# Gate projections of a hybrid attention encoder: 768 full products, or 56 half-size products in two passes

## The chip, the core and the metric

The kernel is one program on one core of a Trainium2 chip. A core has TensorE (PE: matrix products out of SBUF into PSUM), VectorE (DVE), ScalarE (ACT), GpSimd (POOL) and SyncE (SP, which here issues all DMAs). Each engine works through its own list of instructions in order; semaphores hold an instruction back until its inputs are there. Time is device time in microseconds of one execution, the median of several; less is better.

## The reference

One encoder block over 1024 tokens of width 1024 with 16 learned meta tokens put in front (1040 keys), float32. The normed input `h` is projected by `w_in` to the queries, keys and values of two attention branches and to two gates, each 1024 wide:

```
proj = h @ w_in                      # qa ka va | qb kb vb | ga gb
y_a = differential_attention(qa, ka, va)   # 4 heads, all keys, alibi bias; no distance for meta keys
y_b = windowed_gqa(qb, kb, vb)             # 8 heads, window 128 plus the meta keys
merged = sigmoid(ga) * (y_a @ w_ba) + sigmoid(gb) * (y_b @ w_bb)
h = h + merged @ w_o
h = h + (silu(n @ w_gate) * (n @ w_up)) @ w_down,   n = rms_norm(h)
```

Only the 1024 real tokens are returned, so the gates are needed for these alone.

## The kernel before

Every product is made in float32r in three terms: both operands are split into a high part (ACT copies it, rounding) and a low part (DVE or POOL subtracts), and high x high, high x low, low x high are added up in PSUM (`split`, L111). The normed input lies transposed in SBUF as `hT_hi`, `hT_lo` (8 blocks of 128 channels by 1040 tokens) from the start until the gates are done.

**Projections** (L193 to L232, L492 to L533). A column block of `w_in` of 128 columns is loaded (`w_c`), split by ACT and POOL into `wh_c`, `wl_c` (`prep`, L169, two buffers each in `wpool`), and multiplied with the tokens in chunks; a chunk is 8 steps of three matmuls. Results go through `stage` (tile `qk_stage`, three buffers) to HBM, since branch A's operands don't fit beside branch B's. `order` lists the column blocks in the order of use, `ensure` prepares the next one while the present one runs; the 16 gate blocks stand at its end. Branch B (`attend_b`, `units_b`) runs in between, in two groups; the projections of branch A's heads fill PE while a unit of branch B waits for its softmax. In this part the order on all engines is worked out when the program is built, by a planner that goes by the order of writing and by what is ready.

**Branch A and the gates** (L551 to L739). Here PE's order is written out by hand. For each of 4 heads and 8 tiles of 128 queries, `scores_a` makes two score maps in three key chunks (`A_CHUNKS`) each; DVE takes the bias off and keeps the running minimum (L610; the 16 meta keys at the end of the last chunk are a call of their own with `no_dist`), ACT takes the exponential (L615), POOL scales map 1 (L618), DVE joins the maps (L621), POOL copies the meta columns (L622). A tile later the difference is transposed (`transpose_a`), split and multiplied with the values (`values_a`), and each half head is normed (`normed_a`). The gates are the filling: `gate_steps` yields after each step of three matmuls (512 columns each), 8 steps for half a column block, 256 in all; each letter `g` in `SLOTS` (`SLOTS_LAST` for the last head) is one step, 30 (`G_FIRST`) come before head 0 and 10 (`G_HEAD`) before the other heads, to cover `load_a`, and 36 (`HOLD`) are held back for the end. ACT copies each half block out and SP stores it (`g_d`). `gated` (L806) reads them back.

**Pools.** SBUF is given out as two stacks: left `bpool` (branch B), then `apool` (branch A), then `ypool`; right `acon`, `hpool` (hT), `wpool`, `stage`, then `gstage` in the place of `stage`. A pool opened where another was closed takes its memory. Each DMA is one instruction in SP's list.

## Time and profile before

| what | value |
|---|---|
| median of 3 runs | 1461.66 us (1461.31 to 1463.18) |
| profiled execution, its span | 1464.6 us |
| projections and branch B | 66 to 306 us |
| gates alone, loading of head 0 | 306.5 to 327.4 us |
| branch A with gates between | 327.4 to 606 us |
| rest of the gates, last norms | 606 to 642 us |
| merge, output projection, feed-forward | from 642 us |

The profile is of one execution. A row of instructions has the line, the engine, the operation, the tiles (written <- read), shapes and count, then busy time and the mean of one; a median or a mean of a matmul is its whole flight, while matmuls follow one another more closely. Views by window give the busy time of each engine in a stretch; the chain of waits follows the work that ended last backwards, so that its pieces add up to the span. A line can be that of a helper: L112 and L113 are the two halves of every split, L200 every projection's matmul.

### The profile page before, as it was taken

What the parts mean: (1) busy time and instruction counts of PE and PEld (TensorE: products, weight loads), DVE (VectorE), ACT (ScalarE), POOL (GpSimd) and SP (SyncE); (2) the same over time, 40 slices, a digit from 0 to 9 for tenths busy, and PEclk for the clock granted to TensorE, in tenths of its full rate; (3) what the DMA queues carried; (4) which work ended last, traced back from release to release, by engine and by line L of the source; (5) the groups of instructions that cost most, each with busy time, mean ns of one, the idle gap of its engine ahead of it and who ended that gap; (6) DMA issues with size and microseconds to landing.
All of it is one profiled execution on the core that took longest, in us unless ns stands there. A gap on an engine that the chain in (4) does not pass through costs nothing.

```text
span 1464.6 us, 21066 instructions
## 1 busy us (share of the span) xinstructions
PE 1443.4 (99%) x7375; PEld 1238.1 (85%) x7375; DVE 854.9 (58%) x1666; ACT 655.2 (45%) x1237; POOL 534.6 (36%) x502
## 2 busy tenths in 40 slices
PE   8999999999999999999999999999999999999997
PEld 6999989988898999878888878888888888888886
DVE  7355426627786868433513876555555554787667
ACT  6355436525454555444512743333333333444454
POOL 5143223313323232224822565545555442000444
PEclk9999999999999999999999999999999999999999
DMA  7333452372524251077521434323233322954333
GB/s 242 86 95 111 119 131 88 77 209 90 148 77 145 73 153 66 30 261 220 182 106 72 144 109 144 125 98 102 100 108 101 102 100 99 356 188 140 122 127 139
DMA packets 156153, 189.97 MB, mean 130 GB/s; under 512 B 16192, under 2 KB 101632, under 8 KB 156048
## 3 DMA queue, kind: packets, MB, share of 16 engines
q1 hardware_dynamic: 156048, 188.63, 40.5%
q8 instruction: 58, 0.95, 0.3%
q14 instruction: 47, 0.39, 0.1%
HBM read 128.09 MB, written 53.94 MB: 124 GB/s over the span
## 4 chain that ended last, share of the span: by engine, by line
PE 85%; POOL 4%; issue 4%; DMA 3%; DVE 2%; ACT 1%; SPq 1%; POOLq 0%; ACTq 0%; DVEq 0%
PE pg L1092 28%; PE pp_g L200 10%; PE pd L1186 8%; PE po L869 6%; PE ppa L548 4%; PE aps L604 4%; PE apy L646 3%; PE pp_va L200 3%; PE pp_qa L200 3%; PE pp_ka L200 3%; PE pp_qb L200 3%; POOL oa L113 3%; PE apt L633 2%; PE bpt L338 2%; PE bpy L344 2%
## 5 line engine op out<-in xcount | busy, mean ns | idle before, releaser
L1092 PE MATMUL pg<-t,wop 128*128 128x512 f32 x1056 | 242.6, 389 | 0.0
L113 POOL TENSOR_TENSOR wop<-wf,wop 128x512 fp32r<-128x512 f32 x128 | 174.2, 1365 | 164.2 <-ACT wop L112 149.7
L1092 PEld LDWEIGHTS pg<-t,wop 128*128 128x128 f32 x1056 | 198.2, 188 | 41.2
L1186 PE MATMUL pd<-ob,oa 128*128 128x512 f32 x924 | 210.2, 389 | 1.2 <-DVE ob L113 0.7
L1186 PEld LDWEIGHTS pd<-ob,oa 128*128 128x128 f32 x924 | 173.3, 188 | 37.9 <-DVE ob L113 1.2
L1092 PE MATMUL pg<-b,wop 128*128 128x512 f32 x792 | 185.6, 392 | 2.3 <-DVE c L1101 2.3
L1092 PEld LDWEIGHTS pg<-b,wop 128*128 128x128 f32 x792 | 149.4, 189 | 34.2 <-issue 2.4
L113 POOL TENSOR_TENSOR wl_c<-w_c,wh_c 128x1024 fp32r<-128x1024 f32 x32 | 77.6, 2425 | 159.4 <-ACT wh_c L112 134.3
L112 ACT ACTIVATE wop<-wf 128x512 fp32r<-128x512 f32 x128 | 80.3, 632 | 84.2 <-PE pg L1092 52.1
L615 ACT ACTIVATE as<-as,amn 128x1040 f32<-128x1040 f32 x64 | 74.5, 1164 | 73.9 <-DVE amn L610 73.9
L113 POOL TENSOR_TENSOR oa<-ra,oa 128x512 fp32r<-128x512 f32 x33 | 44.0, 1335 | 171.1 <-ACT oa L112 169.7
L200 PE MATMUL pp_g<-hT_hi,wh_c 128*128 128x512 f32 x256 | 101.7, 397 | 0.0
L200 PE MATMUL pp_g<-hT_lo,wh_c 128*128 128x512 f32 x256 | 101.4, 396 | 0.0
L200 PE MATMUL pp_g<-hT_hi,wl_c 128*128 128x512 f32 x256 | 101.3, 396 | 0.0
L112 ACT ACTIVATE oa<-ra 128x512 fp32r<-128x512 f32 x77 | 48.6, 632 | 107.3 <-PE pd L1186 54.6
L604 PE MATMUL aps<-ak,aq 128*128 128x352 f32 (+1 forms) x384 | 93.2, 328 | 0.0
L869 PE MATMUL po<-woh,mT 128*128 128x512 f32 x384 | 88.0, 390 | 0.0
L869 PEld LDWEIGHTS po<-woh,mT 128*128 128x128 f32 x384 | 71.9, 188 | 14.8
L604 PEld LDWEIGHTS aps<-ak,aq 128*128 128x128 f32 x384 | 70.1, 190 | 14.3 <-DVE amn L610 0.2
L927 DVE TENSOR_TENSOR s<-wf,wf 128x512 f32<-128x512 f32 x22 | 18.3, 830 | 107.1 <-DMA wf<-in_w_ff_gate_dram 54.0
L610 DVE CUSTOM_DVE_ANT_0 as<-aps,dist,amn 128x352 f32<-128x352 f32 (+1 forms) x128 | 71.3, 564 | 10.4 <-PE aps L604 8.1
L325 POOL TENSOR_SCALAR bs<-bs,bdn 128x432 f32<-128x432 f32 (+1 forms) x64 | 37.0, 596 | 98.0 <-DVE bdn L323 56.5
(255 smaller groups left out, 2940.4 us busy)
## 6 DMA issues: line engine op xcount, KB each, us to landing
ra<-aop SPq DMA_DIRECT2D x77, 256.0 KB, 2.6
w_c<-in_w_in_dram SPq DMA_DIRECT2D x33, 512.0 KB, 4.0
wf<-in_w_ff_gate_dram SPq DMA_DIRECT2D x24, 512.0 KB, 3.6
wf<-in_w_ff_up_dram SPq DMA_DIRECT2D x24, 512.0 KB, 3.6
aop<-as SPq DMA_DIRECT2D x44, 256.0 KB, 2.1
aop<-c SPq DMA_DIRECT2D x33, 256.0 KB, 2.0
g_d<-gate_stage SPq DMA_DIRECT2D x32, 256.0 KB, 2.0
gt<-g_d SPq DMA_DIRECT2D x32, 256.0 KB, 3.2
```

Of the source, the lines that this page charges most:

```text
L112: nc.scalar.activation(hi, src, AF.Copy)
L113: lo_eng.tensor_tensor(lo, src, f32(hi), ALU.subtract)
L200: nc.tensor.matmul(ps[:, :n], a[:, c, :], b[:, c, at:at + n], start=(c == 0 and i == 0), stop=(c == DC - 1 and i == 2))
L325: nc.gpsimd.tensor_scalar(st[:, r, :W], st[:, r, :W], dn[:, r:r + 1], 1.0, ALU.mult, ALU.mult)
L548: nc.tensor.matmul(ps, w[:, a, j, :], src(j, b, tk), start=(j == 0 and n == 0), stop=(j == 3 and n == 2))
L604: nc.tensor.matmul(ps[:, :n], qs[m][:, t * P:(t + 1) * P], ks[m][:, vv, k0:k0 + n], start=(vv == 0), stop=(vv == 1))
L610: nc.vector.tensor_tensor_reduce(s[m][:, a:b], ps[:, a - k0:b - k0], far_by, slope, low, ALU.add, ALU.min, mn[:, m, i + j:i + j + 1])
L615: nc.scalar.activation(s[m][:, 0:L], s[m][:, 0:L], AF.Exp, bias=low, scale=-1.0, accum_out=dn[:, m:m + 1])
L646: nc.tensor.matmul(py[:, cols], v[:kp, a, k, :], at_[:kp, k, b, :], start=(k == 0 and j == 0), stop=(k == 8))
L869: nc.tensor.matmul(ps, mT[:, c, a, t * P:(t + 1) * P], wos[q, c][:, b], start=(c == 0 and n == 0), stop=(c == DC - 1 and n == 2))
L1092: nc.tensor.matmul(ps, op[:, x, c, :], b[:, y, c, :], start=(p in (1, 2, 5) and c == 0 and n == 0), stop=(p in (4, 2, 3) and c == 3 and n ...
L1186: nc.tensor.matmul(ps[u], oa[:, a, u * P:(u + 1) * P], ob[:, b, :], start=(p in (1, 2, 5) and j == 0 and k == 0), stop=(p in (2, 3, 4) and ...
```

## The change

The gates are made by Winograd's form of Strassen's product: two column blocks (256 columns) of a gate, all 1024 channels and all 1024 tokens are each cut in halves, and seven products of half size (4 steps of 128 channels, three matmuls of 512 columns each) replace eight. The kernel needs sums of weight quarters (POOL, `g_prep`) and sums of token quarters. The latter, 5, 6, 7 and 4, are made once (`token_sums`, on POOL, split by ACT and DVE), in the projections, kept in HBM (`ts_d`) and loaded over quarters of hT that are no longer needed (`load_sums`). Products 2, 5 and 3 of all eight pairs form the first pass and 1, 6, 7 and 4 the second; partial results go to `g_d` and come back (`kept`) to be added by DVE. In all 56 products of 4 steps, 224 steps.

With it go: the gates' weights leave `order`, `wpool` and `stage` are closed before the gates and a new `gpool` takes their place; tiles have four gate steps in all heads; the score chunks become 392, 392 and 256 keys, and the last, with the meta keys in it, uses a copy of the distances with zeros at their place (`dist_m`, made by POOL), so that the separate call goes; the last key projection takes its chunks in reverse order. What is not shown of the diff are the new tiles' declarations in HBM and the removal of `no_dist`.

```diff
@@ -37,11 +37,11 @@
 COMBINE_POOL = (0, 1, 2, 3)
-SLOTS = "sgsgsngsgsgstntnt"
-SLOTS_LAST = "sgsgsngsgsstntnt"
+SLOTS = "sgsgsngsgsstntnt"
 S_BUFS = (2, 2)
...
 G_BUFS = 3
+GV_BUFS = 4
 HOLD = 36
...
@@ -159,7 +161,7 @@
     Q_CHUNKS = [(0, 512), (512, 512)]
-    A_CHUNKS = [(0, 352), (352, 352), (704, 336)]
+    A_CHUNKS = [(0, 392), (392, 392), (784, 256)]
     KB_CHUNKS = [(0, 256), (256, 256), (512, 256), (768, 272)]
@@ -180,7 +182,6 @@
             order += [C_QB + 2 * P, C_QB + 3 * P]
-    order += [C_GB + i * P for i in range(8)] + [C_GA + i * P for i in range(8)]
     prepped = {}
...
@@ -489,6 +488,43 @@
     flush_v()
+    def quad(hl, kh, half):
+        return (hT_hi, hT_lo)[hl][:, 4 * kh:4 * kh + 4, half * 512:half * 512 + 512]
+    tpool, close_tpool = pool("tpool", "right")
+    def token_sums(c):
+        tt = nc.gpsimd.tensor_tensor
+        def new(name):
+            return tpool.tile([P, 512], F32, tag="ta", name=f"ta{name}_{c}", bufs=3)
+        def part(hl, kh, half):
+            return f32(quad(hl, kh, half)[:, c])
+        def keep(p, src):
+            to = tpool.tile([P, 2, 512], F32R, tag="to", name=f"to{p}_{c}", bufs=2)
+            split(to[:, 0], to[:, 1], src, nc.vector)
+            nc.sync.dma_start(ts_d[p][:, :, c, :], f32(to))
+        t1, low = new(1), new("l1")
+        tt(t1, part(0, 0, 1), part(0, 0, 0), ALU.subtract)
+        tt(low, part(1, 0, 1), part(1, 0, 0), ALU.subtract)
+        tt(t1, t1, low, ALU.add)
+        keep(5, t1)
+        t3, t2 = new(3), new(2)
+        tt(t3, part(0, 1, 1), part(0, 0, 1), ALU.subtract)
+        tt(t2, part(1, 1, 1), part(1, 0, 1), ALU.subtract)
+        tt(t3, t3, t2, ALU.add)
+        keep(7, t3)
+        tt(t2, t3, part(0, 0, 0), ALU.add)
+        tt(t2, t2, part(1, 0, 0), ALU.add)
+        keep(6, t2)
+        t4 = new(4)
+        tt(t4, part(0, 1, 0), t2, ALU.subtract)
+        tt(t4, t4, part(1, 1, 0), ALU.add)
+        keep(4, t4)
     def project_a(h):
@@ -509,7 +545,7 @@
         project_v(C_VA + h * P, f"va{h}", va_evac)
-        project(C_KA + h * P, K_CHUNKS, f"ka{h}", evac_split(None, k_consume))
+        project(C_KA + h * P, K_CHUNKS if h < AH - 1 else K_CHUNKS[::-1], f"ka{h}", evac_split(None, k_consume))
@@ -523,8 +559,12 @@
     units_b(0, qb, first_b)
+    for c in range(2):
+        token_sums(c)
     project_a(0)
+    token_sums(2)
     project_a(1)
+    token_sums(3)
     qb = new_qb(1)
@@ -548,21 +588,105 @@
+    close_tpool()
+    close_stage()
+    close_wpool()
+    gpool, close_gpool = pool("gpool", "right")
+    def load_sums(p, kh, half):
+        for hl in range(2):
+            nc.sync.dma_start(f32(quad(hl, kh, half)), ts_d[p][:, hl])
+    load_sums(5, 0, 1)
+    G_ACT = {2: (1, 0), 5: (0, 1), 3: (1, 1), 1: (0, 0), 6: (1, 0), 7: (0, 1), 4: (1, 1)}
+    G_OUT = {2: (0, 0), 5: (1, 1), 3: (0, 1), 1: (0, 0), 6: (0, 1), 7: (1, 1), 4: (1, 0)}
+    order_g = [(2, k) for k in range(4)]
+    for k in range(0, 8, 2):
+        order_g += [(p, k + i) for p in (5, 3) for i in range(2)]
+        if k < 4:
+            order_g += [(2, k + 4 + i) for i in range(2)]
+    for k in range(0, 8, 2):
+        order_g += [(p, k + i) for p in (1, 6, 7, 4) for i in range(2)]
+    g_ready, g_raw, g_kept, g_bank = {}, {}, {}, {}
+    def g_cols(k):
+        return (C_GB, C_GA)[k // 4] + k % 4 * 256
+    def g_tile(name):
+        return gpool.tile([P, 512], F32, tag="gv", name=name, bufs=GV_BUFS)
+    def g_place(p, k):
+        row, half = G_OUT[p]
+        return g_d[2 * k + row][:, half * 512:half * 512 + 512]
+    def g_prep(n):
+        p, k = order_g[n]
+        at, tt = g_cols(k), nc.gpsimd.tensor_tensor
+        def load(out, kh, c0, cn):
+            nc.sync.dma_start(out, w_in[kh * 512:kh * 512 + 512, at + c0:at + c0 + cn].rearrange("(c p) n -> p c n", p=P))
+        if p == 2:
+            src = g_tile(f"g12_{k}").rearrange("p (c n) -> p c n", n=P)
+            load(src, 1, 0, P)
+        else:
+            if p in (5, 1):
+                raw = g_raw[k] = gpool.tile([P, 2, 4, 256], F32, tag="gr", name=f"gr{p}_{k}", bufs=2)
+                load(raw[:, 0], 0, 0, 256)
+                if p == 5:
+                    load(raw[:, 1], 1, 0, 256)
+                else:
+                    nc.sync.dma_start(raw[:, 1, :, 0:P], s2_d[k])
+                    load(raw[:, 1, :, P:256], 1, P, P)
+            raw = g_raw[k]
+            a11, a21, a12, a22 = (raw[:, i, :, j * P:j * P + P] for i in range(2) for j in range(2))
+            if p == 5:
+                tt(a21, a21, a22, ALU.add)
+            elif p == 3:
+                tt(a11, a21, a11, ALU.subtract)
+                nc.sync.dma_start(s2_d[k], a11)
+                tt(a12, a12, a11, ALU.subtract)
+            elif p == 7:
+                tt(a21, a11, a21, ALU.subtract)
+            src = {5: a21, 3: a12, 1: a11, 6: a12, 7: a21, 4: a22}[p]
+            if p in (1, 6, 7):
+                kept = g_kept[p, k] = g_tile(f"gk{p}_{k}")
+                nc.sync.dma_start(kept, g_place(p, k))
+        op = g_ready[p, k] = gpool.tile([P, 2, 4, P], F32R, tag="gop", name=f"gop{p}_{k}", bufs=4)
+        split(op[:, 0], op[:, 1], src, nc.gpsimd)
+    g_prepped = [0]
+    def g_ahead(n):
+        while g_prepped[0] < min(n, len(order_g)):
+            g_prep(g_prepped[0])
+            g_prepped[0] += 1
+    g_ahead(3)
     def gate_steps():
-        for i in range(16):
-            def g_evac(ps, at, n, i=i):
-                st = gstage.tile([P, 512], F32, tag="g", name="gate_stage", bufs=G_BUFS)
-                nc.scalar.copy(st, ps)
-                nc.sync.dma_start(g_d[i][:, at:at + n], st)
-
-            ensure(1)
-            col = (C_GB if i < 8 else C_GA) + (i % 8) * P
-            for _ in project_steps(col, Q_CHUNKS, f"g{i}", g_evac):
+        for n, (p, k) in enumerate(order_g):
+            g_ahead(n + 3)
+            op, act = g_ready.pop((p, k)), G_ACT[p]
+            if p in (2, 5, 1):
+                g_bank[k] = pp_bank(f"pg{p}_{k}")
+            ps = g_bank[k]
+            for c in range(4):
+                for i, (a, b) in enumerate(((0, 0), (0, 1), (1, 0))):
+                    nc.tensor.matmul(ps, op[:, a, c], quad(b, *act)[:, c], start=(p in (2, 5, 1) and c == 0 and i == 0),
+                                     stop=(p in (2, 3, 4) and c == 3 and i == 2), skip_group_check=True)
+                if c == 3:
+                    if p in (1, 6, 7):
+                        st = g_kept.pop((p, k))
+                        nc.vector.tensor_tensor(st, ps, st, ALU.add)
+                    else:
+                        st = gpool.tile([P, 512], F32, tag="g", name="gate_stage", bufs=G_BUFS)
+                        nc.scalar.copy(st, ps)
+                    nc.sync.dma_start(g_place(p, k), st)
+                    if k == 7 and p in (2, 5, 3):
+                        load_sums({2: 6, 5: 7, 3: 4}[p], *act)
                 yield
-            ensure(W_BUFS - 1)
-
-    close_stage()
-    gstage, close_stage = pool("gstage", "right")
     apool, close_apool = pool("apool")
@@ -570,6 +694,12 @@
         nc.gpsimd.memset(s0s[i][:, L + 2 * NM:], 0.0)
+    last_k0 = A_CHUNKS[-1][0]
+    dist_m = apool.tile([P, NT, L - last_k0], F32, name="dist_m")
+    nc.gpsimd.memset(dist_m[:, :, S - last_k0:], 0.0)
+    for t in range(NT):
+        u0 = 896 - t * P
+        nc.gpsimd.tensor_copy(dist_m[:, t, 0:S - last_k0], dist[:, u0 + last_k0:u0 + S])
@@ -603,13 +733,10 @@
                                      start=(vv == 0), stop=(vv == 1))
-                parts = [(k0, min(k0 + n, S), dist[:, u0 + k0:u0 + min(k0 + n, S)])]
-                if k0 + n > S:
-                    parts.insert(0, (S, L, no_dist))
-                for j, (a, b, far_by) in enumerate(parts):
-                    nc.vector.tensor_tensor_reduce(s[m][:, a:b], ps[:, a - k0:b - k0], far_by, slope, low,
-                                                   ALU.add, ALU.min, mn[:, m, i + j:i + j + 1])
-                    low = mn[:, m, i + j:i + j + 1]
+                far_by = dist_m[:, t] if k0 == last_k0 else dist[:, u0 + k0:u0 + k0 + n]
+                nc.vector.tensor_tensor_reduce(s[m][:, k0:k0 + n], ps[:, :n], far_by, slope, low,
+                                               ALU.add, ALU.min, mn[:, m, i:i + 1])
+                low = mn[:, m, i:i + 1]
                 if i < 2:
@@ -671,7 +798,7 @@
-    n_gates = [256 - HOLD]
+    n_gates = [4 * len(order_g) - HOLD]
@@ -715,7 +842,7 @@
             turning = turn(tiles[n - T_LAG])
-        for what in SLOTS if n < 3 * NT else SLOTS_LAST:
+        for what in SLOTS:
             if what == "s":
@@ -739,8 +866,7 @@
     close_psum2()
-    close_stage()
-    close_wpool()
+    close_gpool()
     close_hpool()
```

More of the change, by code (lines that the diff above doesn't have):

```diff
@@ L100, in encoder_block @@
     g_d = [dram.tile([P, S], F32, name=f"g_d{i}") for i in range(16)]
+    ts_d = {p: dram.tile([P, 2, 4, 512], F32, name=f"ts_d{p}") for p in (5, 6, 7, 4)}
+    s2_d = [dram.tile([P, 4, P], F32, name=f"s2_d{k}") for k in range(8)]
     ya_d = [dram.tile([P, S], F32, name=f"ya_d{h}") for h in range(4)]
@@ L465, in encoder_block @@
         nc.gpsimd.memset(tbx[:, j, P:144], 0.0 if j == 1 else FAR)
-    no_dist = acon.tile([P, NM], F32, name="no_dist")
-    nc.gpsimd.memset(no_dist, 0.0)
     far_a = acon.tile([P, 1], F32, name="far_a")
```

## Prediction, written before the changed kernel was run

> **What bounds the kernel now.** I read the page first, for the engine that is never free.
>
> ```profile
> span 1464.6 us, 21066 instructions
> ...
> PE 1443.4 (99%) x7375; PEld 1238.1 (85%) x7375; DVE 854.9 (58%) x1666; ACT 655.2 (45%) x1237; POOL 534.6 (36%) x502
> ...
> PEclk9999999999999999999999999999999999999999
> ```
>
> TensorE (PE) is busy 99% of the span at full clock, so work taken from it is worth its time, and every stall put in front of it costs its time. Then the busy time by stretches (us, then busy us of PE, PE weight loads, DVE, ACT, POOL, the granted clock, DMA share, GB/s), for the two projection stretches before the gates, and the chain of waits for three runs of gate matmuls and for the value matmuls that close each pair of query tiles.
>
> ```profile
> 66.00:178.00 112.00, 111.02 (x667) 101.71 (x666) 61.80 (x148) 60.17 (x145) 34.89 (x46) 1.00 0.39 107
> 178.00:306.00 128.00, 128.00 (x729) 115.48 (x728) 64.19 (x147) 62.92 (x144) 40.02 (x48) 1.00 0.40 107
> 389.77 6.96 PE pp_g L200 x30
> 484.07 1.08 PE apy L646 x9
> 500.41 1.07 PE apy L646 x9
> 570.07 1.07 PE apy L646 x9
> ...
> 600.13 1.08 PE apy L646 x9
> ```
>
> Thirty gate matmuls take 6.96 us on the chain: 0.232 us each, 0.696 us for a gate step of three (the 394 ns of a single record overlaps its neighbours). Two tiles with five gate steps each take 500.41 - 484.07 = 16.34 us; in the last head, with four, four tiles take 600.13 - 570.07 = 30.06. The difference, 8.17 - 7.52 = 0.65 us a tile, is one step: also a tile with four steps is set by TensorE, not by DVE.
>
> Last, the seam between the projections and branch A: the first gate matmuls and the first score matmuls on PE, the DMA issues of SP, and POOL (start, us, line).
>
> ```profile
> 306.50 0.40 PE L200 MATMUL pp_g<-hT_hi,wh_c 128*128 128x512 f32 x1
> ...
> 327.39 0.48 PE L604 MATMUL aps<-ak,aq 128*128 128x352 f32 x2
> 306.17 3.00 SPq L352 DMA_DIRECT2D yb_d<-by  x4
> ...
> 309.97 1.26 SPq L500 DMA_DIRECT2D ka_d<-qk_stage  x2
> 311.32 0.54 SPq L580 DMA_DIRECT2D aq<-qa_d  x1
> 323.78 9.27 DMA w_c<-in_w_in_dram
> 290.76 2.40 POOL L113 TENSOR_TENSOR wl_c<-w_c,wh_c 128x1024 fp32r<-128x1024 f32 x1 [3.36 <-ACT wh_c L112]
> 307.77 2.40 POOL L113 TENSOR_TENSOR wl_c<-w_c,wh_c 128x1024 fp32r<-128x1024 f32 x1 [14.61 <-ACT wh_c L112]
> 310.11 0.27 POOL L572 MEMSET as<- 128x80 f32 x2
> L313 PE MATMUL bps<-kb,qb x128: 288/358/466, 63.8 to 282.1; 128*128 128x432 f32 x96, 128*128 128x288 f32 x32
> q1 hardware_dynamic: 3136, 5.68, 101.6%
> ```
>
> Here PE has no gap: the gates begin as the projections end, because their first weights were split at 290.76 while the last projection ran, in a pool (`wpool`) that lives on; 30 steps (20.9 us) then cover the loading of head 0. But what lies in a newly opened pool starts late. The memset of `as0` stands at 310.11 although POOL idled 14.61 us before 307.77 and the memory was that of `kb0`; `aq` of head 0 is issued at 311.32 although its place was `kb1`, read for the last time near 282.1 (the last score matmul of branch B). A new pool gets its first instruction when the last one of the old pool has gone out, here the `yb_d` stores. And from 311.3 to 331.5 (the last line: packets, MB, share) the DMA engines are full, with 5.68 MB, 281 GB/s; a 512 KB load issued in there at 323.78 takes 9.27 us.
>
> **The change part by part.** *Gate products.* 16 columns x 2 halves x 24 = 768 matmuls become 56 products x 12 = 672: 96 x 0.232 = **-22.3 us** of PE, all of it on the path, since four steps a tile are still PE's. That is 32 gate steps: one fewer in each of 24 tiles of heads 0 to 2, the rest at the end of branch A.
>
> *The seam.* The new `gpool` takes the place of `wpool`, `stage` and `tpool`, so by the two rows above its first load waits for the last `ka_d` store (309.97 + 1.26 = 311.2). Costs of making an operand:
>
> ```profile
> L112 ACT ACTIVATE wop<-wf x128: 615/633/637, 827.9 to 1225.0; 128x512 fp32r<-128x512 f32 x128
> L113 POOL TENSOR_TENSOR wop<-wf,wop x128: 1274/1291/1805, 828.6 to 1225.7; 128x512 fp32r<-128x512 f32 x128
> g_d<-gate_stage SPq DMA_DIRECT2D x32, 256.0 KB, 2.0
> ```
>
> A 256 KB transfer (2.0 to 2.6), ACT's copy 0.63, POOL's rest 1.29 and the hand-overs make 4.7: product (2,0) begins at about 316, where PE was busy from 306.5. Three operands are ordered before `load_a`; (2,3) and the two 1 MB blocks that (5,0) and (5,1) need come behind its 13 issues. Together from 311.3: four 256 KB blocks, 4.1 MB of head 0, 2.1 MB of raw weights, some 1.3 MB of stores: 8.5 MB at 281 GB/s = 30 us, so the last block lands near 341.5. (The token sums' 2 MB go out at about 303, when the reversed K_CHUNKS free their place, into DMA that is idle until 311.) Then POOL has, one behind the other, the sum and split of (5,1), the split of (3,0), and two differences and the split of (3,1): 6 x 1.29 = 7.8; two steps of (3,1) add 1.4. The first scores come at about 351 instead of 327.4: **+23.6 us**. This wait stands at the head of PE's hand-written order, so the scores, whose data have landed, queue behind it. The eight copies that fill `dist_m` (one operand, below 1.29 us each, 10 us in all) fall into POOL's waiting for these loads and cost nothing; without that wait they would. Bounds: 7 us, if only the first operand is late and the rest lands in time; 40 us, if `load_a` goes out wholly before the gate loads, which then start after 331.5 with PE idle till then. I take 23.6, since DMA alone, full, gives it.
>
> *Clock.* PE loses its clock in a wait:
>
> ```profile
> 340.54 1.20 PE L633 MATMUL apt<-ident,as 128*128 128x128 f32 x9 [2.15 <-DVE as L621]
> 342.00:344.00 2.00, 2.00 (x7) 1.71 (x6) 1.86 (x6) 1.62 (x4) 0.38 (x1) 0.50 0.01 1
> 344.00:346.00 2.00, 2.00 (x8) 1.62 (x8) 0.98 (x6) 0.00 (x0) 0.00 (x0) 0.67 0.00 0
> ```
>
> After 2.15 us of idling it ran at 0.50 and 0.67 for 4 us: 2 x 0.50 + 2 x 0.33 = **+1.7 us**, once (a second wait there is followed by more waiting). The Trainium skill, "TensorE: Matmul & The Clock Gate", Part 1, has the clock halved after an idle window of about 3.4 us; the trace shows it after 2.15 us, and by the skill's figure two long waits would cost twice 1.7 us, as an estimate.
>
> *Token sums.* 40 operations on POOL of 1.29 (52 us) and 16 splits on ACT and DVE, in stretches where POOL now works 34.89 + 40.02 of 240 us; 16 stores of 512 KB on SP. They are covered by PE's projections. What is late when POOL is taken are the weight splits that sit behind them; the trace has them ready well ahead:
>
> ```profile
> 73.72 1.95 POOL L325 TENSOR_SCALAR bs<-bs,bdn 128x288 f32<-128x288 f32 x4 [16.50 <-DVE bdn L323]
> 77.87 2.38 POOL L113 TENSOR_TENSOR wl_c<-w_c,wh_c 128x1024 fp32r<-128x1024 f32 x1 [1.85 <-ACT bes L321]
> 90.66 2.09 PE pp_va L200 x12
> ```
>
> 12 of the first 20 fit into POOL's 16.50 us of idleness; the split for `va0` ends at 80.25 and is used at 90.66. They take nothing off the path, so no gain. I take **+2** (0 to 10: one branch B unit's softmax held up by 1.29 us in each of 8).
>
> *Loop of branch A.* DVE's groups (count, busy us, mean ns) in the last head, the addition that resembles the new ones, and the window of two of its tiles:
>
> ```profile
> L610 DVE CUSTOM_DVE_ANT_0 as<-aps,dist,amn 128x352 f32<-128x352 f32 x16 | 9.3, 579 | 2.3 <-PE aps L604 2.0
> L610 DVE CUSTOM_DVE_ANT_0 as<-aps,dist,amn 128x320 f32<-128x320 f32 x16 | 8.8, 547 | 0.3
> L610 DVE DVE_READ_ACCUMULATOR2_ANT amn<- 128x1 f32 x64 | 5.2, 82 | 0.0
> L610 DVE CUSTOM_DVE_ANT_0 as<-aps,no_dist,amn 128x16 f32<-128x16 f32 x16 | 3.7, 229 | 1.3 <-PE aps L604 0.4
> L1106 DVE TENSOR_TENSOR p<-pg,p 128x512 f32<-128x512 f32 x21 | 14.4, 686 | 6.2 <-PE pg L1092 4.7 <-ACT p L1112 1.5
> 572.00:587.00 15.00, 15.00 (x102) 13.95 (x101) 12.98 (x44) 8.25 (x14) 3.08 (x5) 1.00 0.07 24
> ```
>
> 1 ns a column: chunks of 392, 392, 256 cost 619 + 619 + 483 and three reads, where 579 + 579 + 547 + 229 and four stood; 0.3 us less per map, 0.6 per tile. The 24 additions of the second pass (686 ns, one operand in PSUM) put 0.5 back in half of the tiles. DVE stays at its 13 of 15 us. POOL gets one product a tile, 1.29 to 3.9 us; it works 3 of 15 now. With the gates' loads and stores between, and four steps instead of five over each head's loading, DVE's relief gains nothing where PE sets the tile, but it pays for the wait of `L622` or `L618` behind one more POOL operation. I take **+3** (0 to 12) over 32 tiles.
>
> *Tail.* 36 steps are left where 40 were, in front of branch B's loads:
>
> ```profile
> 631.99 9.26 DMA tb<-yb_d
> 642.68 44.29 PE ppa L548 x194
> ```
>
> The load lands at 641.2 and PE goes on at 642.7: the 4 steps saved (2.8 us) are mostly waited out, **+2** (0 to 2.8).
>
> Sum: 1464.6 - 22.3 + 23.6 + 1.7 + 2 + 3 + 2 = 1474.6 for the profiled execution; its span is 2.9 above the median of the runs, 1461.66, so 1471.7.
>
> **Rivals.** *The seam is bridged (faster).* If the order of SP puts the raw blocks of (5,0) and (5,1) ahead of head 0's, or the pool opens earlier, PE loses only the first operand, 7 to 10 us: 1461.66 - 22.3 + 9.6 + 1.7 + 2 + 1 + 2 = 1455.7. For it: weights of g1 and g2 were loaded before `load_a` in the old kernel, whose order follows readiness. Against: those lay in an open pool. It decides where the seam costs under 14 us.
>
> *A wash.* The seam costs 14 to 18: 1461.
>
> *Head 0 first.* The gate loads go out behind all of `load_a`; 40 instead of 23.6: 1488.
>
> *Branch A's loop is no longer PE's.* `L621` reads two SBUF tiles, and has never met POOL at its start; another such operation has:
>
> ```profile
> L621 DVE SCALAR_TENSOR_TENSOR as<-as,adn,as x32: 1280/1298/1304, 339.2 to 603.7; 128x1040 f32<-128x1040 f32 x32
> L1108 DVE TENSOR_TENSOR c<-c,p x22: 680/1744/1810, 844.2 to 1236.7; 128x512 f32<-128x512 f32 x22
> ```
>
> 680 alone, 1810 beside POOL's splits: up to 1.13 us more. Above 0.9 a tile, DVE (6.6 of 7.5 us) is full and PE waits; half of it in 32 tiles, 18 us instead of 3: 1487. The Trainium skill, "GPSIMD Engine Reference", 8. Key points, says that POOL shares its SBUF interfaces with DVE and contends with DVE instructions of two SBUF inputs; the rows agree.
>
> **How the numbers follow.** Forecast (seam of 18 to 32 us) 0.49, of which nearly all is slower; bridged 0.24; wash 0.09; head 0 first 0.10; loop 0.08. No change means within 0.2% (2.9 us), which is what a measurement here can tell. Faster 0.24, same 0.09, slower 0.67. The forecast's own range is 1466 to 1481; 1450 (bridged, nearly free) to 1489 (head 0 first) holds 8 in 10.
>
> **What would show it.** Right: PE idle near 306 to 316 and again before (5,0), released by POOL's `gop` splits, these by DMA of `gr`; first `aps` matmul 20 us or more after the last `pp_ka` than now; the tiles at 7.5 us; 672 gate matmuls at 0.232. Wrong: gate matmuls straight behind the last `pp_ka`; raw blocks issued before `aq`; gaps on PE between 66 and 306; tiles over 7.8 us with DVE's `L621` near 2 us.

## The result, and the profile after

The changed kernel takes 1505.5 us (median of 4 runs, 1502.5 to 1507.7) where the kernel before takes 1461.7 beside it: 1.029 times as long, 95% interval 1.0277 to 1.0303. Forecast was 1471.7 with a range to 1489. The sign was right; the size, 10 us instead of 43.7, was less than a quarter. The profiled execution has a span of 1500.8 us, 36.2 more than before's; it lies 4.7 below the median of its runs, and before's lay 2.9 above, which makes up the rest of the 43.7. (A measured time is some 1.8 us more than the span of the same execution, so the profiled execution of the kernel before is itself some 4.7 us slower than its median.)

The page of the changed kernel, first its engines and clock by slices, then the chain that ended last by engine:

```profile
span 1500.8 us, 21142 instructions
PE 1434.8 (96%) x7279; PEld 1227.3 (82%) x7279; DVE 884.2 (59%) x1578; ACT 680.3 (45%) x1293; POOL 674.6 (45%) x622
PEclk9999999978999999989999999999999999999999
DMA packets 184570, 231.92 MB, mean 155 GB/s; under 512 B 17984, under 2 KB 115712, under 8 KB 184464
PE 68%; DMA 10%; POOL 9%; issue 5%; DVE 5%; ACT 2%; SPq 1%; POOLq 0%; DVEq 0%; ACTq 0%
```

PE is busy 96% of a longer span, at a lower clock in three slices, and a fifth of the chain is now DMA and POOL (7% before). What PE waited for between 300 and 640 us (us in total, times, longest), in the kernel before and in the changed one:

```profile
PE apt L633 <- DVE as L621: 2.2, 1, 2.2
```

```profile
PE pg L676 <- ACT gop L114: 19.6, 3, 15.6
PE apt L760 <- DVE as L748: 8.8, 4, 4.5
PE apt L760 <- POOL as L749: 4.3, 2, 2.7
PE aps L734 <- DVE amn L737: 2.2, 4, 1.4
PE aps L734 <- DMA ak<-ka_d: 1.0, 1, 1.0
PE pg L676 <- POOL gop L115: 1.0, 1, 1.0
PE aps L734 <- DVE at L764: 0.5, 1, 0.5
```

Two groups: gate products that wait for their operands (the seam), and transposes and scores that wait for a tile's own softmax steps (the loop). The end adds a third, 8.4 us of the first branch product on `yb`. By stages, from the first and last instructions of each in the two traces (the last gate product and the first branch product by their starts; work left out at 0.696 us a step):

| stage | before | after | difference | work left out | lost |
|---|---|---|---|---|---|
| to the last key projection | 306.7 | 306.7 | 0.1 | | 0.1 |
| seam: to the first scores | 20.7 | 47.6 | +26.9 | | 26.9 |
| loop: to the last tile's first scores | 266.5 | 269.1 | +2.7 | 24 steps, 16.7 | 19.4 |
| to the last gate product | 45.2 | 41.3 | -3.9 | 8 steps, 5.6 | 1.7 |
| to the first branch product | 0.2 | 8.8 | +8.6 | | 8.6 |
| the rest | 825.3 | 827.3 | +1.9 | | 1.9 |

**The seam** in the changed kernel: first SP's issues (start, us, line).

```profile
311.06 0.60 SPq L710 DMA_DIRECT2D aq<-qa_d  x1
...
313.05 3.08 SPq L627 DMA_DIRECT2D g<-in_w_in_dram  x3
...
324.49 5.19 SPq L627 DMA_DIRECT2D gr<-in_w_in_dram  x2
```

The first gate matmul on PE, with its idle time and releaser:

```profile
322.30 0.79 PE L676 MATMUL pg<-hT_hi,gop 128*128 128x512 f32 x1 [15.56 <-ACT gop L114]
```

And pieces of the chain:

```profile
306.81 5.25 DMA hT_hi<-ts_d
...
325.80 12.77 DMA gr<-in_w_in_dram
...
338.72 1.28 POOL gr L644
```

As forecast, no gate load goes out before the last key store, and the raw blocks go out behind most of head 0's loads; the one on the chain takes 12.77 us. Unforeseen: three of head 0's loads are even ahead of the first gate loads, and SP holds the second of these three until the token sums' transfer of 5.25 us has landed at 312.06.

**The loop.** POOL's order in head 1 (start, us, in brackets the idle time before and its releaser):

```profile
440.21 1.29 POOL L644 TENSOR_TENSOR gr<-gr 128x512 f32<-128x512 f32 x1 [8.29 <-DMA gr<-in_w_in_dram]
441.44 0.21 POOL L749 COPY as<-as 128x32 f32<-128x32 f32 x1
...
452.67 1.26 POOL L648 TENSOR_TENSOR gr<-gr 128x512 f32<-128x512 f32 x1
453.88 0.20 POOL L749 COPY as<-as 128x32 f32<-128x32 f32 x1
```

A transpose on PE in head 0:

```profile
372.99 0.48 PE L760 MATMUL apt<-ident,as 128*128 128x128 f32 x1 [2.75 <-POOL as L749]
```

And two operations with count and shortest, median and longest duration in ns:

```profile
L749 POOL COPY as<-as x32: 199/209/1222, 371.7 to 633.4; 128x32 f32<-128x32 f32 x32
L748 DVE SCALAR_TENSOR_TENSOR as<-as,adn,as x32: 1280/1301/2446, 365.9 to 632.1; 128x1040 f32<-128x1040 f32 x32
```

POOL sat 8.29 us in front of a weight sum whose block had not landed (the block's load took 11.43 us beside head 1's loads), with the tile's 0.2 us copy behind it in its order. Ten operations later the next copy comes out at 453.88, and the transposes of that tile wait for it.

The waits are not all of the loop's loss. PE idles 15.5 us in the loop (2.2 in the kernel before), and behind the long waits it ran for a while at half clock, which costs it another 5.4 us (1.7 before; the rows stand in the part on the clock below). Together that is 17.0 of the 19.4 us; the other 2.4 were not followed up.

### The profile page after: what moved, and what is told of

Read it like the earlier page. It is cut to its first block, busy times and chain, and to the rows that moved or that the text cites. A ratio compares the mean times of both kernels' runs of the same rounds, so it can differ in the third digit from the quotient of the medians.

```text
span 1500.8 us, 21142 instructions
## 1 busy us (share of the span) xinstructions
PE 1434.8 (96%) x7279; PEld 1227.3 (82%) x7279; DVE 884.2 (59%) x1578; ACT 680.3 (45%) x1293; POOL 674.6 (45%) x622
## 4 chain that ended last, share of the span: by engine, by line
PE 68%; DMA 10%; POOL 9%; issue 5%; DVE 5%; ACT 2%; SPq 1%; POOLq 0%; DVEq 0%; ACTq 0%
PE pg L1218 26%; PE pd L1312 8%; PE po L995 5%; PE pg L676 5%; PE ppa L588 4%; DMA gr<-in_w_in_dram 4%; PE pp_qb L201 3%; POOL oa L115 3%; PE aps L734 2%; PE pp_va L201 2%; DMA ak<-ka_d 2%; PE pp_qa L201 2%; PE apy L773 2%; PE pp_ka L201 2%; PE bpt L339 1%
## 5 line engine op out<-in xcount | busy, mean ns | idle before, releaser
L676 PE MATMUL pg<-hT_hi,gop 128*128 128x512 f32 x448 | 168.7, 408 | 20.8 <-ACT gop L114 19.6
L676 PEld LDWEIGHTS pg<-hT_hi,gop 128*128 128x128 f32 x448 | 87.0, 195 | 38.1 <-ACT gop L114 20.8
L734 PE MATMUL aps<-ak,aq 128*128 128x392 f32 (+1 forms) x384 | 91.2, 332 | 3.8 <-DVE amn L737 2.2
L742 ACT ACTIVATE as<-as,amn 128x1040 f32<-128x1040 f32 x64 | 74.5, 1164 | 43.4 <-DVE amn L737 39.6
L676 PE MATMUL pg<-hT_lo,gop 128*128 128x512 f32 x224 | 90.8, 405 | 0.0
L1053 DVE TENSOR_TENSOR s<-wf,wf 128x512 f32<-128x512 f32 x22 | 27.0, 1228 | 104.5 <-DMA wf<-in_w_ff_gate_dram 56.6
L115 POOL TENSOR_TENSOR gop<-gr,gop 128x512 fp32r<-128x512 f32 x48 | 66.9, 1396 | 41.0 <-ACT gop L114 37.9
L737 DVE CUSTOM_DVE_ANT_0 as<-aps,dist,far_a 128x392 f32<-128x392 f32 x64 | 39.5, 618 | 62.8 <-PE aps L734 62.4
```

Source lines behind the costliest of these rows:

```text
L115: lo_eng.tensor_tensor(lo, src, f32(hi), ALU.subtract)
L676: nc.tensor.matmul(ps, op[:, a, c], quad(b, *act)[:, c], start=(p in (2, 5, 1) and c == 0 and i == 0), stop=(p in (2, 3, 4) and c == 3 and ...
L734: nc.tensor.matmul(ps[:, :n], qs[m][:, t * P:(t + 1) * P], ks[m][:, vv, k0:k0 + n], start=(vv == 0), stop=(vv == 1))
L737: nc.vector.tensor_tensor_reduce(s[m][:, k0:k0 + n], ps[:, :n], far_by, slope, low, ALU.add, ALU.min, mn[:, m, i:i + 1])
L742: nc.scalar.activation(s[m][:, 0:L], s[m][:, 0:L], AF.Exp, bias=low, scale=-1.0, accum_out=dn[:, m:m + 1])
```

## Experiments

Times are medians; where a number is set against 1505.5 it is the changed kernel's. Edits are shown in part.

### One part alone: the score chunks

```diff
-    A_CHUNKS = [(0, 352), (352, 352), (704, 336)]
+    A_CHUNKS = [(0, 392), (392, 392), (784, 256)]
...
+    dist_m = apool.tile([P, NT, L - last_k0], F32, name="dist_m")
```

> The kernel before, with the score chunks of the change alone (392, 392, 256 keys, meta keys in the last with the copied distances); nothing is left out. By the prediction DVE's relief (0.6 us a tile) is worth nothing where PE sets the tile, and the eight copies on POOL and their 8 KB cost nothing: 1461.7, within 3 us either way. A rival: the shorter chain of DVE calls after the last score product ends the waits of the tiles' transposes earlier, 0.2 us in each of 32 tiles, 5 to 7 us faster.

Measured: 1462.6 beside 1463.2, ratio 0.9999 (0.999 to 1.0008). The prediction's reading holds for the old kernel, with the old gates: the relief of DVE and the eight copies are worth nothing there.

### The seam: first operand early, or fewer steps ahead of the scores

```diff
-        return gpool.tile([P, 512], F32, tag="gv", name=name, bufs=GV_BUFS)
+        if not g_half:
+            g_half.append(wpool.tile([P, DC, P], F32, tag="w", name=name, bufs=2))
+            return g_half[0][:, 0:4]
+        return g_half.pop()[:, 4:8]
...
-        op = g_ready[p, k] = gpool.tile([P, 2, 4, P], F32R, tag="gop", name=f"gop{p}_{k}", bufs=4)
+        op = g_ready[p, k] = wpool.tile([P, DC, P], F32R, tag=("wh", "wl")[n % 2], name=f"gop{p}_{k}", bufs=W_BUFS).rearrange("p (a c) n -> p a c n", a=2)
```

> Gate operands (16 KB) and their 256 KB inputs (8 KB) lie in the projections' pool, which stays open; only the raw blocks (gr) and the gate's output tiles lie in the new pool. Nothing is left out. Both theories: PE has no gap at 306.7 us and products (2,0) to (2,3) run to about 318 us. Theory D (the DMA queue sets the end of the seam; the raw blocks go out behind head 0's loads and land near 340 us): the gap returns before (5,0), first scores at 348 to 352 instead of 354.3, the median 2 to 6 us lower. Rival E (the late opening of the pool at the first operand sets it): first scores near 339, the median 15 us lower.

Measured: 1497.6. The first gate matmul starts at 306.1 without a gap, and the wait moves whole to (5,0): first scores at 351.4. PE's longest wait in this run, then pieces of its chain:

```profile
PE pg L679 <- ACT gop L114: 19.2, 1, 19.2
```

```profile
320.03 10.88 DMA g_d<-gate_stage
330.93 7.27 DMA gr<-in_w_in_dram
```

So the late pool accounts for 3 of the 27 us; transfers in a full queue account for the end. For the seam this is theory D, as in the prediction. The median fell by 7.8 us, more than theory D's 2 to 6: head 0 takes 65.7 us instead of 71.7, for which no run here separates a reason.

```diff
-G_FIRST = 30
+G_FIRST = 16
```

> 16 gate steps instead of 30 ahead of head 0's scores; the other 14 come after the last head. Nothing is left out. Theory D: head 0's keys and queries have landed by 332 us, so the first scores start when (2,3) is through, near 338 us; the waits before (5,0) and (5,1) and (3,1), 3.5 + 0.5 + 2.0 us, go, the median falls by 4 to 8 us. Tail: 14 more gate steps (9.7 us) lie over branch B's loads. Theory F (branch B's splits wait until the gates' pool is given back, which is when the last gate tile is stored): PE still idles about 8.6 us before the first branch product. Rival G (the loads lack cover): that wait is gone, and 8 us more are gained.

Measured: 1494.2, first scores at 342.4. Theory D holds, with more gained (11.3 us) than expected, though the scores start 4 us later than forecast. At the end, 14 more steps did not cover the wait; of 8.4 us 6.65 remain (the first branch product on PE):

```profile
664.69 3.74 PE L588 MATMUL ppa<-yb,wbhb 128*128 128x512 f32 x7 [6.65 <-ACT yb L114]
```

That speaks for theory F.

### The loop: what the tiles' steps stand behind

```diff
-        nc.gpsimd.tensor_copy(s[0][:, L:L + 2 * NM].rearrange("p (a k) -> p a k", a=2),
+        nc.vector.tensor_copy(s[0][:, L:L + 2 * NM].rearrange("p (a k) -> p a k", a=2),
```

> Only the copy of the meta columns (the 128x32 copy behind DVE's joining of the maps) goes from POOL to DVE; nothing is left out. Theory A (the tiles' own POOL steps stand in POOL's order behind gate operands that wait for their loads): the transposes' waits at 368, 373, 450 and 454 us (4.65, 3.04, 2.26, 1.87 us) become shorter, heads 0 and 1 lose 4 to 8 us, the median falls from 1505.5 to 1496 to 1501. Rival B (the gates' extra DMA traffic makes gate operands late for PE itself): no change, within 3 us.

Measured: 1501.5 (1497.1 to 1504.5): heads 0 and 1 together 3.6 us shorter. That is between the two forecasts, a little less than theory A's least and more than rival B's 3 us; the range overlaps that of the changed kernel, so by time alone the gain is hardly clear of the noise. PE no longer waits for POOL's copy, but 7.6 us remain on DVE's joining of the maps, which waited in part (1.9 us) for POOL's scaling.

```diff
-                (nc.gpsimd if t % 4 in COMBINE_POOL else nc.vector).tensor_scalar(
-                    s[1][:, 0:L], s[1][:, 0:L], dn[:, 1:2], neglam, ALU.mult, ALU.mult)
+                nc.vector.tensor_tensor(dn[:, 1:2], dn[:, 1:2], neglam, ALU.mult)
+                nc.scalar.activation(s[1][:, 0:L], s[1][:, 0:L], AF.Copy, scale=dn[:, 1:2])
```

> As the run with the copy on DVE, and POOL's scaling of map 1 (1.2 us a tile) goes to ACT, with its factor made by a tiny DVE product; nothing of a tile but the norm's small step is left to POOL. Theory A: heads 0 and 1 lose nearly all of the 16 us they are over their four-step time, the median falls to 1488 to 1493. Rival B: no change against the run with the copy alone. Rival C (ACT's order, which has the gates' splits in it too, takes POOL's place): as slow as before or slower, with the transposes' waits released by ACT.

Measured: 1506.4, nothing gained. Head 0 falls to 65.0 us (from 71.7), but head 2 rises to 73.7 (from 69.3). ACT in head 2 of this run:

```profile
502.10 0.63 ACT L114 ACTIVATE gop<-gr 128x512 fp32r<-128x512 f32 x1 [8.62 <-DMA gr<-in_w_in_dram]
502.63 1.15 ACT L742 ACTIVATE as<-as,amn 128x1040 f32<-128x1040 f32 x1
```

The same picture on another engine: the first half of a gate split waits for its load, and an exponential that the tile needs stands behind it. By its time this is rival C, but not by the sign that it named: PE's waits are still released by DVE (the longest of its waits on DVE's minimum is now 3.6 us), which at 503.90 had itself idled 4.66 us for that exponential. The fault is not POOL's alone.

```diff
-            if p == 5:
-                tt(a21, a21, a22, ALU.add)
...
-                tt(a12, a12, a11, ALU.subtract)
```

> The changed kernel with the 32 sums and differences of weight quarters left out (the products take the raw quarters): 41 us of POOL less, all loads and stores as in the changed kernel. If POOL's working time is what holds the tiles' steps up, the loop loses nearly all of its 16 to 19 us (1486 to 1490), and the seam 3 to 4 us besides. If it is the in-order queues standing behind preparations that wait for their loads, head 0, where POOL works without a break, loses its 8 us, and heads 1 and 2 keep 8 of their 10: 1490 to 1496.

```diff
             if p in (5, 1):
-                raw = g_raw[k] = gpool.tile([P, 2, 4, 256], F32, tag="gr", name=f"gr{p}_{k}", bufs=2)
-                load(raw[:, 0], 0, 0, 256)
...
+                if p == 5 and k < 2:
+                    raw = g_raw[k] = gpool.tile([P, 2, 4, 256], F32, tag="gr", name=f"gr{p}_{k}", bufs=2)
...
+                g_raw[k] = g_raw[k % 2]
```

> The changed kernel with the raw blocks of the first pair used for all pairs: 24 of 32 block loads and 8 reloads of the kept difference are left out (some 9.4 MB), all POOL, ACT and DVE work stays. If preparations that wait for loads hold up the engines' queues, the waits in heads 1 and 2 go (450 and 454 us, 10.8 us in a tile) while head 0 keeps at least 5 of its 8 us: 8 to 12 us faster, 1493 to 1498. If POOL's working time does it, heads 1 and 2 stay as they are: within 3 us of 1505.

Measured: 1485.6 without the sums, 1490.3 without the loads. Windows of about head 0 and head 1 (us; busy us of PE, weight loads, DVE, ACT, POOL; clock, DMA share, GB/s), in the changed kernel, without sums, and without loads:

```profile
355.00:426.00 71.00, 62.72 (x354) 55.66 (x353) 52.19 (x143) 40.03 (x75) 44.57 (x40) 0.93 0.46 148
426.00:500.00 74.00, 69.30 (x417) 62.63 (x416) 54.98 (x152) 41.91 (x79) 40.03 (x38) 0.95 0.79 252
```

```profile
355.00:426.00 71.00, 67.26 (x398) 59.60 (x396) 52.42 (x153) 42.56 (x80) 28.86 (x29) 1.00 0.63 193
426.00:500.00 74.00, 73.78 (x461) 67.06 (x460) 60.38 (x171) 44.72 (x86) 31.04 (x33) 1.00 0.82 272
```

```profile
355.00:426.00 71.00, 65.00 (x370) 58.50 (x369) 54.70 (x145) 42.22 (x79) 50.35 (x47) 0.95 0.35 114
426.00:500.00 74.00, 73.99 (x465) 67.73 (x465) 57.88 (x166) 44.19 (x83) 33.69 (x35) 1.00 0.63 212
```

From one head's first scores to the next one's, heads 0, 1 and 2 take 71.7, 74.5 and 69.3 us in the changed kernel, 61.7, 71.1 and 67.5 without sums, and 68.3, 67.1 and 67.5 without loads. So POOL's work is what holds head 0 (in its window POOL is busy for 28.86 instead of 44.57 us and PE for 67.26 instead of 62.72), and the loads are what hold head 1 (PE is busy for 73.99 of 74 us with all sums still there). A part of both gains is the clock, 1.00 in these two windows where the changed kernel has 0.93 and 0.95. From the first scores to the last tile's, the loop shrinks from 269.1 us to 254.4 and 255.4, by 14.7 and 13.7: together more than the 19.4 lost. So they are not two terms side by side. A reading that fits, though no run isolates it: a late load turns POOL's sums into a bunch, and the tile's steps stand behind the bunch; with less of either, it is short or early enough. Neither of the two theories was right alone: without the sums heads 1 and 2 lost 5.2 us, where waiting queues alone would have left them 8 of their 10, and without the loads they lost 9.2, where POOL's working time alone would have left them as they are. Both runs came out faster than forecast.

### The end

```diff
-GT_BUFS = 4
-WB_BUFS = 5
+GT_BUFS = 2
+WB_BUFS = 4
```

> Two smaller buffer counts in the merge (weights 4 instead of 5, gate halves 2 instead of 4), by which branch B's split tiles come to lie below the gates' pool instead of 7 KB inside it; nothing is left out. Theory F (the splits wait until the gates' pool is given back by the store of the last gate tile): the 8.6 us of idling before the first branch product shrink to below 3; fewer buffers may give some of it back in the merge: the median 4 to 7 us lower. Rival G (the loads of branch B land too late): the idling stays at 8 us or more and the median at 1505.

Measured: 1497.1, 8.3 less and a little more than forecast, and PE's wait ahead of the first branch product goes from 8.4 us to 0.2. The chain in the changed kernel, then ACT in this run:

```profile
667.77 5.05 DMA g_d<-gate_stage
...
672.87 0.62 ACT yb L114
...
673.54 0.80 PE ppa L588
```

```profile
666.79 1.15 ACT L114 ACTIVATE yb<-tb 128x512 fp32r<-128x512 f32 x2
...
669.42 0.57 ACT L684 COPY gate_stage<-pg 128x512 f32<-128x512 f32 x1
```

Theory F holds. By the kernel's memory plan the new pool reaches 10 KB further down than the projections' `stage` did, so that 7 KB of branch B's last split tile lie in it; all eight splits then stand behind the last gate store (they run from 672.87 on, when it has landed). Moved clear of it, four run before the last gate copy and four straight behind it, with no store to wait for.

### Mending several at once

To the operands' place, the 16 steps and the copy on DVE comes a pool for the gates' output tiles:

```diff
+    gout, close_gout = pool("gout", "right")
     gpool, close_gpool = pool("gpool", "right")
...
-                        st = gpool.tile([P, 512], F32, tag="g", name="gate_stage", bufs=G_BUFS)
+                        st = gout.tile([P, 512], F32, tag="g", name="gate_stage", bufs=G_BUFS)
```

> Four mends in one, nothing left out: gate operands in the pool that stays open, 16 steps ahead of head 0, the copy of the meta columns on DVE, and the gates' output tiles in a pool of their own so that branch B's splits wait for the raw blocks' pool only. If the causes found are separate and add up: seam first scores near 330 us (24 us earlier than 354.3, of which 10 are steps moved to the end), so 14 us gained; 4 from the copy; 8 from the tail: 1505.5 - 26 = 1479, range 1473 to 1486. If they are one cause counted twice (late loads that are then waited for in the first tiles), above 1488.

Measured: 1488.9, the second case: one cause counted twice. First scores at 322.9, but the first tile takes 20.3 us, since PE waits there 12.5 us for the same gate operand.

```diff
-    order_g = [(2, k) for k in range(4)]
+    order_g = [(2, k) for k in range(8)]
...
-            g_ahead(n + 3)
+            g_ahead(n + 4)
```

> As the four mends together, and the products ordered by what they need: all eight products 2, which need one 256 KB load and no sum, first (20 steps ahead of head 0, 12 in its first three tiles), their loads ahead of head 0's; operands prepared four products ahead instead of three. Nothing is left out. If the loss is operands that come too late for the order in which they are used, the raw blocks now have until about 345 us, the first scores start near 325 us, head 0 runs at its four-step time and heads 1 and 2 lose half of theirs: 1455 to 1466. If the loop's loss is the engines' work itself, not below 1475.

Measured: 1472.1, 33.4 us better than the change, short of the first forecast, but below what the second allows, so the engines' work is not the whole of the loop's loss. The raw blocks are no longer waited for; PE waits for output tiles instead (ACT, then PE's waits):

```profile
334.13 1.24 ACT L696 COPY gate_stage<-pg 128x512 f32<-128x512 f32 x2 [10.53 <-DMA g_d<-gate_stage]
```

```profile
PE pg L688 <- ACT gate_stage L696: 11.9, 2, 8.8
```

```diff
+                            two = f32(stage.tile([P, 2, 512], F32R, tag="qk", name="gate_stage", bufs=QK_BUFS))
+                            g_outs[:] = [two[:, 1], two[:, 0]]
+                        st = g_outs.pop()
```

> As the run with the products ordered by need, with two differences: the gates' output tiles are halves of the projections' staging tiles (six instead of three, in a pool that stays open), which needs the 8 KB of the copied distances, so the score chunks are the old ones (352, 352, 336 and a call for the meta keys); and 24 steps instead of 20 ahead of head 0. Nothing is left out. If the waits at 315.5 us (3.3 us, the output tile's pool opening behind the last key store) and at 334.8 us (8.9 us, three output tiles whose stores take 11.65 us beside head 0's loads) are what is left of the seam, both go, with 1 to 2 us of low clock: 1457 to 1461, the first scores near 325 us and tile 0 at 5 to 8 us instead of 15.9. If another transfer of the same burst takes their place (the raw blocks, landing near 340 us), tile 1 or 2 waits instead and the time stays above 1465.

Measured: 1474.9, the second forecast. The waits for output tiles are gone and tile 0 takes 6.8 us, but tile 1 takes 10.9, as in the rival. The old chunks came back in the same kernel, so what each did isn't separated.

```diff
+                if not h:
+                    fill(12)
                 ld = load_a(h)
-                fill(G_HEAD if h else G_FIRST)
+                fill(G_HEAD if h else G_FIRST - 12)
```

> As the run with the products ordered by need (with the new score chunks), and: the pool of the gates' output tiles lies where the token sums' pool was, so that it opens when these are stored; the first 12 gate steps stand ahead of head 0's loads in the order of writing, so that the stores of their results stand between those loads; and the two smaller buffer counts in the merge that keep branch B's splits clear of that pool. Nothing is left out. If output tiles stuck behind head 0's loads are what is left of the seam, the waits of 3.3 and 8.9 us go and 2 us come back in the merge: 1458 to 1464 instead of 1472. If DMA itself, full until about 340 us, sets the end, tile 0 to 2 keep 8 us or more of waiting, on outputs, on raw blocks or on the value loads: 1466 or more.

Measured: 1466.8, the second forecast and the best form: 1.0025 (1.001 to 1.0039) of the kernel before, so still not faster. PE's largest wait, and the window behind the first scores:

```profile
PE aps L746 <- DMA ak<-ka_d: 8.3, 5, 2.2
```

```profile
322.00:330.00 8.00, 5.30 (x15) 4.32 (x16) 1.59 (x5) 1.70 (x3) 1.26 (x1) 0.57 1.05 285
```

Now head 0's and head 1's keys themselves are late, in a DMA queue that is full.

Against that kernel:

```diff
-G_HEAD = 10
-G_FIRST = 20
+G_HEAD = 12
+G_FIRST = 24
```

> As the run with the early fill, with 24 steps instead of 20 ahead of head 0's scores and 12 instead of 10 ahead of the other heads'; ten steps fewer are left for the end. Nothing is left out. If what is left of the loss is PE waiting for keys and queries at the heads' beginnings (322.6, 325.2, 331.8, 402.5 us: 2.1, 2.5, 1.5, 2.5 us), steps put there are worth up to 6 us: 1459 to 1464. If the waits only move (to the raw blocks, which land near 340 us, or to the end, where ten steps fewer cover branch B's loads): 1466 to 1470.

Measured: 1474.4, slower than either forecast. Scores now wait 0.7 us for keys, but 18 us of waits remain, spread over output tiles, softmax steps and operands. More cover at the heads only moved them; no version here beats the kernel before.

## Why the prediction was wrong, step by step

- *Gate products, -22.3:* right. The chain still has 9 of them in 2.10 us, 0.233 each, and 96 are gone. That four steps leave a tile to PE is right too where nothing is late: without the loads head 1 takes 67.1 us, and 72.2 before less eight steps are 66.6.
- *Seam, +23.6 (7 to 40):* right in mechanism and nearly in size: 23.6, or 25.3 with the clock's 1.7, against 26.9. DMA moved 8.50 MB at 280 GB/s from 311.3 to 341.6 us (forecast 8.5 at 281), and the last raw block landed at 341.6 (341.5). The steps behind it took 12.7 us, not 9.2, so the scores began at 354.3 (351). The first operand came at 322 and not 316: its 256 KB load went out at 313.05, not 311.3, and took 8.5 us in the full queue, not 2.0. That didn't move the end, as the run with the operands in the open pool shows: DMA, not the pool, sets it.
- *Clock, +1.7, once:* too small. Five stretches in which the changed kernel's clock was at one half:

```profile
308.80:325.80 17.00, 3.37 (x7) 2.26 (x8) 0.00 (x0) 1.89 (x3) 2.97 (x3) 0.50 1.03 277
336.20:342.80 6.60, 6.47 (x14) 4.46 (x15) 0.00 (x0) 1.05 (x2) 5.27 (x5) 0.50 1.12 330
366.90:376.90 10.00, 5.88 (x19) 5.00 (x20) 5.59 (x10) 1.47 (x3) 6.24 (x6) 0.50 0.34 105
452.20:458.80 6.60, 5.02 (x16) 4.09 (x15) 4.21 (x12) 3.16 (x6) 6.60 (x7) 0.50 0.57 159
667.30:677.30 10.00, 3.75 (x8) 2.62 (x9) 4.94 (x9) 8.11 (x15) 0.00 (x0) 0.50 1.05 351
```

  They begin in or behind waits of PE of 15.6, 3.4, 4.5, 2.1 and 8.4 us. At half clock three gate matmuls take 1.28 us (in the kernel before, at 342.09) instead of 0.70, so about half of PE's busy time in these rows is lost: 1.7 and 3.2 us in the seam, 2.9 and 2.5 in the loop, 1.9 behind the first branch product. In the seam, where the prediction put its 1.7, this hardly lengthens the path, as PE waited again behind each of the two, for 3.4 us and for 0.7 and 1.0; behind most of the other 7.3 us no wait follows, and the prediction has nothing for them. The Trainium skill, "TensorE: Matmul & The Clock Gate", Part 1, has the clock halved after an idle window of about 3.4 us; the stretch at 452.2 came behind 2.1 us of idling, like the one behind 2.15 us in the kernel before, so here the measurement goes against that figure.
- *Token sums, +2 (0 to 10):* cost nothing on PE's path; the last key projection ends at 306.74, in the kernel before at 306.67. Their reload, though, is on the chain of the seam.
- *Loop, +3 (0 to 12):* **the step that failed.** It priced what POOL adds ("one product a tile, 1.29 to 3.9 us; it works 3 of 15 now") as work, and found room for it. It cost 19.4 us (3.7 of them more low clock than before), outside its bounds, because an engine's order is a queue: the prediction named `L622` and `L618` as standing behind one more operation, but not that this operation may wait 8 us for its load, nor that ten may come at a time. The kernel before shows the same thing once, at the load that the prediction's last seam row has at 323.78; ACT there:

```profile
333.15 1.06 ACT L112 ACTIVATE wh_c<-w_c 128x1024 fp32r<-128x1024 f32 x1 [9.15 <-DMA w_c<-in_w_in_dram]
334.12 0.57 ACT L555 COPY gate_stage<-pp_g 128x512 f32<-128x512 f32 x1
334.58 1.17 ACT L615 ACTIVATE as<-as,amn 128x1040 f32<-128x1040 f32 x1
```

  A gate split waits 9.15 us for its block, a tile's exponential stands behind it, and the chain goes on from there, over DVE, to the wait of 2.15 us from which the prediction read its clock term. It did not ask what that wait stood behind. In the changed kernel an operand's load goes out only when the product two before it begins, eight steps or two tiles ahead; the ten steps ahead of each head use that up. Removing the loads, or the sums, gave 14 us back; moving two tile steps to other engines gave 4 us and then none, for ACT's order has the gates' splits in it too.
- *Tail, +2 (0 to 2.8):* wrong cause. The row at 642.68 is only where the chain passes to PE: in the kernel before the first branch product starts at 639.3, and PE waits 0.5 us for it. The steps saved there did matter little; the 8.6 us come from the placing of the new pool, whose late release the prediction used at the seam and didn't apply at the other end.
- *Nothing for the rest:* 1.9 us more from the first branch product on. That is what the half clock behind the 8.4 us of waiting costs, by the last row above.

The sum's miss of 26.3 us in the profiled execution is 16.4 + 1.7 of the loop and what follows, 6.6 of the tail, 1.6 of the seam with its clock and 1.9 of the rest, less 1.9 of the token sums. Of the rivals, none happened. The bridged seam failed by 13 us. The wash has a slip in it: by the prediction's own sum a seam of 14 to 18 us gives 1462 to 1466, not 1461. "Branch A's loop is no longer PE's" gave nearly the right amount (18), and that is luck, as its reason is a small part of the loss: its sign, `L748` near 2 us, shows in single tiles only, and the median is 1301 ns, as before. Two of these tiles do stand right in front of PE's waits of 4.5 and 2.1 us; there DVE took 2289 and 2446 ns, about 1 us too long each.

## What to carry to other kernels

When work is moved onto an engine that is mostly idle, look at what its operations wait for, not only at how long they run: each one that waits for a transfer stops everything behind it in that engine's order, on ACT as on POOL, and a long wait of PE costs clock on top. Compare the lead of the operands with the longest transfer in the fullest stretch (here 12 us or more; two products, 8 x 0.696 = 5.6 us, were the lead in the seam). That a longer lead alone would make the smaller number of products pay is not shown: the best form here is still no faster than the kernel before. And a pool put in another's place gates at both ends: look where its memory ends up and who gets it next.

## What was not expected of the hardware

- A load of 256 KB that took 2.0 to 2.6 us on its own took 8.5 us at the seam, and in the run ordered by need a store of 256 KB took 11.65, with DMA full: transfers in a burst all land late, and changing their order hardly moved the last one (the last of the four raw blocks landed at 341.6 in the changed kernel and at 340.9 in the run ordered by need).
- The 128x32 copy of the meta columns takes POOL 209 ns. On DVE it took 173 (median of the run with the copy alone moved), but in head 0 of the run ordered by need, with POOL's sums beside it, 574 on average, and DVE's joining of two maps 1688 instead of 1301 (count, busy us, mean ns, then idle time before):

```profile
L760 DVE SCALAR_TENSOR_TENSOR as<-as,adn,as 128x1040 f32<-128x1040 f32 x8 | 13.5, 1688 | 2.6 <-POOL as L757 2.2
L761 DVE COPY as<-as 128x32 f32<-128x32 f32 x8 | 4.6, 574 | 0.0
```

  The Trainium skill, "GPSIMD Engine Reference", 8. Key points, has POOL contend with DVE instructions in a 2-port mode or of two SBUF inputs; the first row agrees. The copy has one input, and no run here shows whether it was in such a mode.
